# Combining two expert outputs per token: no zeroes ahead of the first store, and the first two tokens stored by themselves

## The chip, the cores and the metric

The kernel runs on one core of a Trainium2 chip. The metric is the device time of one execution in microseconds (us). Three runs of the kernel before took 238.85, 238.95 and 239.05 us, a median of 238.95. Smaller is better.

## The reference

Each of 16 x 1024 tokens has two rows of 512 float32 numbers (one from each of two experts) and two weights. The result is the weighted sum of the two rows:

```python
batch, seq, hidden, n_experts, k = 16, 1024, 512, 8, 2
# expert_outputs: (batch, seq, k, hidden), combine_weights: (batch, seq, k)
weights = combine_weights[..., np.newaxis]
return np.sum(expert_outputs * weights, axis=2).astype(np.float32)
```

Per token that is 4 KB in, 2 KB out, two multiplications and one addition for each output number. Over 16384 tokens 67.1 MB are read and 33.6 MB are written.

## The kernel before

**Tiling.** The tokens lie 128 to a "column": every one of the 128 partitions handles 128 tokens of its own. Those 128 are cut into ten tiles of `TILES = [13, 13, 12, 13, 13, 13, 12, 13, 13, 13]` tokens per partition. Tokens 0 to 114 of a partition are neighbours in memory (`main` is 115); the last tile's 13 come from a second region of the tensor. On the chip there is one large buffer, `et`, with four rooms (13, 13, 12 and 13 tokens a partition). Tile g goes into room g modulo 4, so it can be loaded when what was stored from that room has left it. `halves` is a second view of the same buffer in units of one 512-number row; a token takes two such rows.

**Order.** It is written out by hand; no planner changes it. There are two DMA queues here. The one that SyncE issues for (q1 in the profile; the profile writes SP for SyncE) takes all loads of expert outputs (line 76) and the last two stores. The one that ScalarE issues for (q10; ACT) takes the weights and the first seven stores (line 130). The start is:

1. VectorE clears `zt`, 16 x 128 numbers (line 108), and ScalarE issues a DMA that writes those 8 KB of zeroes to 16 places spread over the output (line 111). The stores overwrite them later.
2. ScalarE issues the weights: one DMA of 115 KB for tokens 0 to 114 (line 79) and two of 6.5 KB for the last tile (line 114). Then it loads its function table with one small operation (line 115).
3. Beside that SyncE issues the loads of the first four tiles, in five pieces, `FIRST = [2, 11, 13, 12, 13]`: two tokens, then the other eleven of tile 0, then tiles 1, 2 and 3. The first piece is cut into runs of 4 KB (`max_dma_last_dim`), so that each of its DMA rows is 4 KB long; in the others a row is all that a partition gets, 44 to 52 KB.

**Steps of a tile.** For tiles 0 to 7 (`WHOLE`) VectorE multiplies the whole room by the weights, in place (line 88), and then adds the two rows of each token into the front half of the room (line 97). The ScalarE queue then issues the store of the room, and SyncE the load of the tile four later, which waits until that store has landed. Tile 8 (`MIXED`) shares the products: VectorE takes the second row of all 13 tokens and the first row of three (lines 94 and 96), ScalarE the first row of the other ten (line 92). Tiles 7 and 8 leave in one store of 6.5 MB, whose issue waits for the sum of tile 8. The last tile goes token by token, ScalarE multiplying (line 102) and VectorE multiplying and adding (line 103), and leaves in the last store.

In this text L1 to L11 are the eleven loads in the order of their issue (L1: two tokens, L2: eleven, L3 to L11: tiles 1 to 9), S0 to S6 the stores of tiles 0 to 6, S78 that of tiles 7 and 8, and S9 the last.

**Semaphores.** The framework gives the DMAs eight semaphores in turn; a DMA that gets one that is still in use waits for the earlier owner. L5 gets that of the zeroes.

Of the kernel before, what the change touches and what calls it, by code (L numbers as in the profile page):

```python
# [1 line left out]

# [4 lines left out]


@with_exitstack
def kernel(  # L10
    ctx: ExitStack,  # L11
    tc: tile.TileContext,
    expert_outputs: bass.AP,
    combine_weights: bass.AP,
    out: bass.AP,
):

    nc = tc.nc
    b, s, k, h = expert_outputs.shape
    assert k == 2
    n = b * s
    P = nc.NUM_PARTITIONS
    per = n // P
    assert per * P == n

    ROOM = [13, 13, 12, 13]
    ROOMS = len(ROOM)  # L30
    SITE = [sum(ROOM[:i]) for i in range(ROOMS)]
    TILES = [13, 13, 12, 13, 13, 13, 12, 13, 13, 13]
    FIRST = [2, 11, 13, 12, 13]
    STORES = [[0], [1], [2], [3], [4], [5], [6], [7, 8], [9]]
    WHOLE = [0, 1, 2, 3, 4, 5, 6, 7]
    MIXED = [8]
    ALONE = 3
    FREE = {9: 0}
    LAST = 13
    assert all(c <= ROOM[g % ROOMS] for g, c in enumerate(TILES))  # L40
    assert sum(TILES) == per and [g for st in STORES for g in st] == list(range(len(TILES)))
    main = per - LAST
    starts = [sum(TILES[:g]) for g in range(len(TILES))]

    def rows(x):

        first = x[0 : P * main, :].rearrange("(p t) f -> p t f", p=P)
        second = x[P * main : n, :].rearrange("(p t) f -> p t f", p=P)
        return lambda t, c: first[:, t : t + c, :] if t < main else second[:, t - main : t - main + c, :]

    flat = out.rearrange("b s h -> (b s) h")
    eo = rows(expert_outputs.rearrange("b s k h -> (b s) (k h)"))
    cw = rows(combine_weights.rearrange("b s k -> (b s) k"))
    o = rows(flat)

    dt = mybir.dt.float32
    mult = mybir.AluOpType.mult
    add = mybir.AluOpType.add
    copy = mybir.ActivationFunctionType.Copy

    pool = ctx.enter_context(tc.tile_pool(name="all", bufs=1))
    et = pool.tile([P, sum(ROOM), k * h], dt)
    halves = et.rearrange("p j (k h) -> p (j k) h", k=k)
    wt = pool.tile([P, per * k], dt)
    wk = wt.rearrange("p (t k) -> p t k", k=k)
    zt = pool.tile([16, 128], dt)
    warm = pool.tile([P, 1], dt)

    def place(t):
        g = max(g for g in range(len(TILES)) if starts[g] <= t)  # L70
        return SITE[g % ROOMS] + t - starts[g]

    def load(t, c, **kw):
        at = place(t)
        assert place(t + c - 1) == at + c - 1
        nc.sync.dma_start(out=et[:, at : at + c], in_=eo(t, c), **kw)  # L76

    def weights(q, t, c):
        q.dma_start(out=wk[:, t : t + c, :], in_=cw(t, c))

    def combine(g, base):
        at, c, t0 = SITE[g % ROOMS], TILES[g], starts[g]
        if g in WHOLE or g in MIXED:
            room = halves[:, k * at : k * (at + c), :]
            x0, x1 = et[:, at : at + c, 0:h], et[:, at : at + c, h : 2 * h]
            if g in WHOLE:
                wb = wt[:, k * t0 : k * (t0 + c)].unsqueeze(2).to_broadcast([P, k * c, h])
                nc.vector.tensor_tensor(out=room, in0=room, in1=wb, op=mult)  # L88
            else:
                for i in range(ALONE, c):  # L90
                    x = et[:, at + i, 0:h]
                    nc.scalar.activation(out=x, in_=x, func=copy, scale=wt[:, k * (t0 + i) : k * (t0 + i) + 1])  # L92
                w1 = wk[:, t0 : t0 + c, 1:2].to_broadcast([P, c, h])
                nc.vector.tensor_tensor(out=x1, in0=x1, in1=w1, op=mult)  # L94
                w0 = wk[:, t0 : t0 + ALONE, 0:1].to_broadcast([P, ALONE, h])
                nc.vector.tensor_tensor(out=x0[:, 0:ALONE], in0=x0[:, 0:ALONE], in1=w0, op=mult)  # L96
            nc.vector.tensor_tensor(out=halves[:, base : base + c, :], in0=x0, in1=x1, op=add)  # L97
            return
        for i in range(c):
            t = k * (t0 + i)  # L100
            x0, x1 = halves[:, k * (at + i), :], halves[:, k * (at + i) + 1, :]
            nc.scalar.activation(out=x0, in_=x0, func=copy, scale=wt[:, t : t + 1])  # L102
            nc.vector.scalar_tensor_tensor(  # L103
                out=halves[:, base + i, :], in0=x1, scalar=wt[:, t + 1 : t + 2], in1=x0, op0=mult, op1=add
            )

    with tc.manual_schedule():
        nc.vector.memset(zt, 0.0)  # L108

        ahead = flat[0 : P * main, :].rearrange("(q t) h -> q (t h)", q=16)  # L110
        nc.scalar.dma_start(out=ahead[:, 0:128], in_=zt)  # L111
        weights(nc.scalar, 0, main)
        for half in (slice(0, P // 2), slice(P // 2, P)):
            nc.scalar.dma_start(out=wk[half, main:per, :], in_=cw(main, per - main)[half])
        nc.scalar.activation(out=warm, in_=nc.const_aps.tensor(1.0, (P, 1), dt), func=copy)  # L115

        t = 0
        for i, c in enumerate(FIRST):
            load(t, c, **({"max_dma_last_dim": k * h * 4} if i == 0 else {}))
            t += c  # L120
        assert t == sum(TILES[:ROOMS])
        for j, st in enumerate(STORES):
            room = FREE.get(st[0], st[0] % ROOMS)
            base, c = SITE[room] * k, 0
            for g in st:
                combine(g, base + c)
                c += TILES[g]
            assert c <= k * ROOM[room]
            q = nc.sync if j in (7, 8) else nc.scalar
            q.dma_start(out=o(starts[st[0]], c), in_=halves[:, base : base + c, :])  # L130
            for g in st:
                if g + ROOMS < len(TILES):
                    load(starts[g + ROOMS], TILES[g + ROOMS])


# [1 line left out]
_INS = ['expert_outputs', 'combine_weights']  # L137
_OUTS = [((16, 1024, 512), 'float32')]


# [23 lines left out]
```

## Time and profile before

| what | us |
|---|---|
| median of three runs (238.85 to 239.05) | 238.95 |
| profiled execution, its span (its own total time is not listed beside it) | 237.1 |
| VectorE busy | 190.0 (80% of the span) |
| ScalarE busy | 15.8 (7%) |
| both DMA queues, share of the 16 DMA engines over the span | 75.9% + 23.0% |
| moved | 100.80 MB, 425 GB/s over the span |

The span is what the profiler saw between the first and the last instruction; what lies around it is 1.85 us, taken against the median of the runs. In the table by windows, the DMA share counts a DMA row (the profile calls it a packet) wholly in the window in which it starts. A window that is short beside a row can therefore show more than 1, or much less; a window that begins and ends where rows of all 16 engines do is exact. "Landing" is the time from the issue of a DMA to the last of its semaphore's updates.

### The profile page before, as it was taken

To read this page: it belongs to the slowest core of one execution; us is meant where nothing else is said; L and a number is where in the kernel's file an instruction comes from. 1 tells how busy PE (TensorE), PEld (TensorE's weight loads), DVE (VectorE), ACT (ScalarE), POOL (GpSimd) and SP (SyncE) were. 2 spreads that over 40 slices of the span, in tenths; PEclk is the share of its full clock that TensorE was granted. 3 is DMA by queue.
4 is the path that set the end of the run, shared out by engine and by line. 5 is a ranking of instruction groups with operands and counts; after the bars stand their busy time and mean duration, and the time that the engine had idled before them with its cause. 6 is when DMAs were issued, how large, how long until landed. Compare 5 with 4: busy or idle time off the path is not lost.

```text
span 237.1 us, 154 instructions
## 1 busy us (share of the span) xinstructions
DVE 190.0 (80%) x33; ACT 15.8 (7%) x25; POOL 0.2 (0%) x4
## 2 busy tenths in 40 slices
DVE  0006999999999999999999998998499969919400
ACT  2000000000000000000000000000000055019200
POOL 0000000000000000000000000000000000000000
DMA  8999999989999999999899999999899999899996
GB/s 300 388 481 434 432 421 398 470 348 485 449 431 458 431 440 390 486 420 420 359 492 409 409 509 392 431 503 431 359 431 503 420 397 483 381 431 431 431 431 287
DMA packets 3344, 100.80 MB, mean 425 GB/s; under 512 B 512, under 2 KB 656, under 8 KB 912
## 3 DMA queue, kind: packets, MB, share of 16 engines
q1 hardware_dynamic: 2000, 77.33, 75.9%
q10 hardware_dynamic: 1344, 23.47, 23.0%
HBM read 67.24 MB, written 33.56 MB: 425 GB/s over the span
## 4 chain that ended last, share of the span: by engine, by line
DVE 55%; DMA 36%; issue 1%; ACT 0%; DVEq 0%; ACTq 0%; SPq 0%
DVE et L88 35%; DVE et L97 17%; DMA out_dram<-et 17%; DMA et<-in_expert_outputs_dram 12%; DMA wt<-in_combine_weights_dram 8%; DVE et L103 3%; ACT et L102 0%; DVEq L159 0%; ACTq L111 0%; DVE zt L108 0%; DVEq L88 0%; SPq L76 0%; ACTq L102 0%
## 5 line engine op out<-in xcount | busy, mean ns | idle before, releaser
L88 DVE TENSOR_TENSOR et<-et,wt 128x13312 f32<-128x13312 f32 (+1 forms) x8 | 110.0, 13754 | 23.8 <-DMA wt<-in_combine_weights_dram 18.7
L97 DVE TENSOR_TENSOR et<-et 128x6656 f32<-128x6656 f32 (+1 forms) x9 | 62.8, 6973 | 0.4
L92 ACT ACTIVATE et<-et,wt 128x512 f32<-128x512 f32 x10 | 6.2, 708 | 188.0 <-DMA et<-in_expert_outputs_dram 188.0
L103 DVE SCALAR_TENSOR_TENSOR et<-et,wt 128x512 f32<-128x512 f32 x13 | 8.7, 747 | 5.0 <-ACT et L102 5.0
L102 ACT ACTIVATE et<-et,wt 128x512 f32<-128x512 f32 x13 | 8.1, 707 | 14.0 <-DMA et<-in_expert_outputs_dram 14.0
L94 DVE TENSOR_TENSOR et<-et,wt 128x6656 f32<-128x6656 f32 x1 | 7.1, 7093 | 2.3 <-DMA et<-in_expert_outputs_dram 2.3
L96 DVE TENSOR_TENSOR et<-et,wt 128x1536 f32<-128x1536 f32 x1 | 1.8, 1751 | 0.0
L115 ACT ACT_TABLE_LOAD x1 | 1.3, 1283 | 3.1 <-issue 3.1
L108 DVE MEMSET zt<- 16x128 f32 x1 | 0.2, 165 | 0.8 <-PEq L148 0.8
L115 ACT ACTIVATE warm<-const-float32-1.0 128x1 f32<-128x1 f32 x1 | 0.2, 203 | 0.0
L148 POOL MEMSET const-bfloat16-1.0<- 128x1 bf16 x1 | 0.1, 102 | 0.0
L148 POOL MEMSET const-uint8-127<- 128x1 uint8 x1 | 0.1, 101 | 0.0
L148 POOL MEMSET const-float32-0.0<- 128x1 f32 x1 | 0.1, 99 | 0.2 <-issue 0.2
L148 POOL MEMSET const-float32-1.0<- 128x1 f32 x1 | 0.1, 98 | 0.0
## 6 DMA issues: line engine op xcount, KB each, us to landing
et<-in_expert_outputs_dram SPq DMA_DIRECT2D x7, 6656.0 KB, 32.2
out_dram<-et ACTq DMA_DIRECT2D x5, 3328.0 KB, 34.7
et<-in_expert_outputs_dram SPq DMA_DIRECT2D x2, 6144.0 KB, 41.1
out_dram<-et SPq DMA_DIRECT2D x1, 6656.0 KB, 19.9
out_dram<-et ACTq DMA_DIRECT2D x2, 3072.0 KB, 37.2
et<-in_expert_outputs_dram SPq DMA_DIRECT2D x1, 5632.0 KB, 18.2
out_dram<-et SPq DMA_DIRECT2D x1, 3328.0 KB, 14.0
et<-in_expert_outputs_dram SPq DMA_DIRECT2D x1, 1024.0 KB, 5.0
```

The costliest lines, as they stand in the source:

```text
L88: nc.vector.tensor_tensor(out=room, in0=room, in1=wb, op=mult)
L92: nc.scalar.activation(out=x, in_=x, func=copy, scale=wt[:, k * (t0 + i) : k * (t0 + i) + 1])
L94: nc.vector.tensor_tensor(out=x1, in0=x1, in1=w1, op=mult)
L96: nc.vector.tensor_tensor(out=x0[:, 0:ALONE], in0=x0[:, 0:ALONE], in1=w0, op=mult)
L97: nc.vector.tensor_tensor(out=halves[:, base : base + c, :], in0=x0, in1=x1, op=add)
L102: nc.scalar.activation(out=x0, in_=x0, func=copy, scale=wt[:, t : t + 1])
L103: nc.vector.scalar_tensor_tensor(out=halves[:, base + i, :], in0=x1, scalar=wt[:, t + 1 : t + 2], in1=x0, op0=mult, op1=add)
L108: nc.vector.memset(zt, 0.0)
L115: nc.scalar.activation(out=warm, in_=nc.const_aps.tensor(1.0, (P, 1), dt), func=copy)
L148: nc = _bacc.Bacc("TRN2", target_bir_lowering=False, num_devices=1)
```

## The change

It does four things. The buffer `zt`, its clearing and the DMA of zeroes go. ScalarE's first instruction is now the DMA of the weights. Ahead of the loop over tiles, the two tokens of L1 are multiplied, added and stored by themselves, the store through the ScalarE queue. For tile 0 the loop then multiplies, adds and stores the other eleven tokens only. The helpers `products`, `sums` and `store` hold what was written out before; for the tiles from 1 on they issue the same instructions.

```diff
-    zt = pool.tile([16, 128], dt)
...
+    def products(room, t, c):
+        wb = wt[:, k * t : k * (t + c)].unsqueeze(2).to_broadcast([P, k * c, h])
+        nc.vector.tensor_tensor(out=room, in0=room, in1=wb, op=mult)
+
+    def sums(at, c, base):
+        x0, x1 = et[:, at : at + c, 0:h], et[:, at : at + c, h : 2 * h]
+        nc.vector.tensor_tensor(out=halves[:, base : base + c, :], in0=x0, in1=x1, op=add)
+
+    def combine(g, base, done=0):
+        at, c, t0 = SITE[g % ROOMS] + done, TILES[g] - done, starts[g] + done
+        if g in WHOLE:
+            products(halves[:, k * at : k * (at + c), :], t0, c)
+            sums(at, c, base)
+            return
...
+    def store(q, t, base, c):
+        q.dma_start(out=o(t, c), in_=halves[:, base : base + c, :])
+
     with tc.manual_schedule():
-        nc.vector.memset(zt, 0.0)
-
-        ahead = flat[0 : P * main, :].rearrange("(q t) h -> q (t h)", q=16)
-        nc.scalar.dma_start(out=ahead[:, 0:128], in_=zt)
         weights(nc.scalar, 0, main)
...
+        early = FIRST[0]
+        products(halves[:, k * SITE[0] : k * (SITE[0] + early), :], 0, early)
+        sums(SITE[0], early, k * SITE[0])
+        store(nc.scalar, 0, k * SITE[0], early)
         for j, st in enumerate(STORES):
             room = FREE.get(st[0], st[0] % ROOMS)
             base, c = SITE[room] * k, 0
+            done = early if j == 0 else 0
             for g in st:
-                combine(g, base + c)
+                combine(g, base + c + done, done)
                 c += TILES[g]
             assert c <= k * ROOM[room]
-            q = nc.sync if j in (7, 8) else nc.scalar
-            q.dma_start(out=o(starts[st[0]], c), in_=halves[:, base : base + c, :])
+            store(nc.sync if j in (7, 8) else nc.scalar, starts[st[0]] + done, base + done, c - done)
```

More of the change, by code (lines that the diff above doesn't have):

```diff
@@ L79, in weights @@
         q.dma_start(out=wk[:, t : t + c, :], in_=cw(t, c))
[L81 to L84, printed above, removed]
-            x0, x1 = et[:, at : at + c, 0:h], et[:, at : at + c, h : 2 * h]
[L86 to L97, printed above, removed]
+    def products(room, t, c):
+        wb = wt[:, k * t : k * (t + c)].unsqueeze(2).to_broadcast([P, k * c, h])
+        nc.vector.tensor_tensor(out=room, in0=room, in1=wb, op=mult)
```

9 lines of the change are left out of this document (added).

## The prediction

> **What bounds the kernel now.** I read first the 40 slices with the DMA rows, then the chain that ended last, then the DMA engines by windows, then the landings. On the profile's page:
>
> ```profile
> DVE  0006999999999999999999998998499969919400
> DMA  8999999989999999999899999999899999899996
> q1 hardware_dynamic: 2000, 77.33, 75.9%
> q10 hardware_dynamic: 1344, 23.47, 23.0%
> DVE 55%; DMA 36%; issue 1%; ACT 0%; DVEq 0%; ACTq 0%; SPq 0%
> ```
>
> The chain gives 55% to VectorE, and would make it the bound. The slices say otherwise: VectorE has holes from the middle on, the DMA engines have none, and the two queues together fill 98.9% of 16 engines' time. The chain goes through VectorE only because each tile passes it. The DMA engines by windows, chosen so that rows of all engines begin and end at the edges (columns: window, its length, busy time of VectorE, ScalarE, GpSimd with counts, clock, DMA share, GB/s):
>
> ```profile
> 0.00:1.81 1.81, 0.17 (x1) 0.00 (x0) 0.20 (x4) 1.00 0.00 0
> 1.81:3.00 1.19, 0.00 (x0) 0.00 (x0) 0.00 (x0) 1.00 0.96 158
> 3.00:5.00 2.00, 0.00 (x0) 1.49 (x2) 0.00 (x0) 1.00 1.01 410
> 41.65:43.49 1.84, 1.84 (x1) 0.00 (x0) 0.00 (x0) 1.00 0.99 427
> 43.49:45.74 2.25, 2.25 (x1) 0.00 (x0) 0.00 (x0) 1.00 0.98 350
> 51.60:206.20 154.60, 146.92 (x17) 6.23 (x10) 0.00 (x0) 1.00 1.00 433
> 212.05:227.70 15.65, 8.71 (x13) 8.07 (x13) 0.00 (x0) 1.00 1.01 436
> 227.75:235.65 7.90, 0.00 (x0) 0.00 (x0) 0.00 (x0) 1.00 1.00 431
> 235.65:237.10 1.45, 0.00 (x0) 0.00 (x0) 0.00 (x0) 1.00 0.01 0
> ```
>
> From 51.60 to 235.65 us they are busy without a break at 431 to 436 GB/s, loads, stores or both. What is lost lies in four places: 1.81 us ahead of the first byte; a cold start, 1.19 us at 158 GB/s, which at 433 would take 0.43, so 0.75 us lost; 0.41 us (2.25 against 1.84) in the one round of rows of L4 just ahead of the first rows of S0, the first large store; 1.45 us behind the last byte. So the time is bytes over rate plus these four. VectorE's lead counts only where the DMA engines would run out of issued transfers.
>
> **The change part by part.** The rows on which the terms rest, in the order start, DMA issues, landings, VectorE:
>
> ```profile
> 0.73 4.52 SPq L76 DMA_DIRECT2D et<-in_expert_outputs_dram  x5
> 1.01 0.39 ACTq L111 DMA_DIRECT2D out_dram<-zt  x1
> 1.43 0.45 ACTq L79 DMA_DIRECT2D wt<-in_combine_weights_dram  x1
> L76 SPq DMA_DIRECT2D et<-in_expert_outputs_dram x11: 327/328/643, 0.7 to 183.9; - x11
> et<-in_expert_outputs_dram SPq DMA_DIRECT2D x1, 1024.0 KB, 5.0
> et<-in_expert_outputs_dram SPq DMA_DIRECT2D x1, 5632.0 KB, 18.2
> wt<-in_combine_weights_dram ACTq DMA_DIRECT2D x1, 115.0 KB, 18.2
> out_dram<-zt ACTq DMA_DIRECT2D x1, 8.0 KB, 3.9
> 19.73 14.04 DVE et L88
> 33.78 7.09 DVE et L97
> ```
>
> *Zeroes gone.* 8 KB at 433 GB/s are 0.02 us of DMA time. The clearing (0.17 us) was on an idle VectorE. L5's issue waited for the zeroes to land, at 1.01 + 3.9 = 4.9 us; it is now issued some 2 us sooner, worth nothing, since L2 to L4 (16.6 MB, 38 us at 433) are queued ahead of it. Sum: -0.02.
>
> *Weights first.* They move from 1.43 to about 0.73, beside L1's issue. Today their 115 KB need 18.2 us because each of their rows waits behind a row of L2 (a partition's 44 KB, 5632 KB over 128, take 1.66 us on one engine at 433/16 GB/s; eight per engine, 13 us). Now their eight rows per engine stand among L1's sixteen of 4 KB (0.16 us each at 410/16), so they should land with L1, at about 6 us. The bytes are the same. Two costs are not shown anywhere. First, two queues issue in the same moment: loads' issues took 0.33 to 0.64 us, so L1's may come up to 0.3 late with everything behind it, or not at all; I take 0.1, because L1 is likely to be past its issue before the other queue presses. Second, the cold start may be paid again for a second tensor: from 0 to +0.75, the loss in the window 1.81 to 3.00; below nothing by as much as 0.3, if two queues overlap their first latencies. I take 0, nearest to the rows after it, where L2 and the zeroes joined without a dip that the rates show (3.00:5.00 at 410).
>
> *Two tokens early.* VectorE: 2/13 of 14.04 and of 7.09, so 2.16 + 1.09 = 3.25 us, from about 6 to 9.4 us, where it idles today until 19.73. If that cover were gone (weights late, rival 4) it would cost nothing more than now, since the same 3.25 us are then inside tile 0. The store's issue follows on ScalarE's queue, where nothing waits behind it until S0; it is the ninth DMA, and the semaphore that it takes over is that of one of the first, all landed by then but for the weights in rival 4. On the DMA engines its 512 KB leave S0, so the bytes stay; as rows of 4 KB they go at 410 GB/s in place of 433: 1.28 - 1.21 = +0.07.
>
> *First large store.* The dip of 0.41 us ahead of S0 belongs, by place, to the first rows that are written in bulk; the zeroes ahead of it, 8 KB, did not prevent it. It should move to the early store, at about 10 us, among rows of L2. Bounds: -0.41 (small rows do not cause it, and S0 is then no longer the first) to +0.41 (paid at both). I take 0.
>
> *Tile 0 shorter.* It begins when L2 has landed, now at 19.73, then later by the early rows passed before it, about 5 of 8 per engine (0.8 us), and sooner by what the weights trail L2 today (at most 0.2): 20.4. Eleven thirteenths of 21.13 are 17.9 us, so S0 is issued at 38.3 where it was at 40.9. VectorE is then 2.6 us ahead, and S0, shorter by 2/13, lands about 4 us sooner. On busy DMA engines this buys nothing; it only changes who goes first. What it changes at the end is the next step.
>
> *Who is late next: S78.* The two queues alternate row by row, so stores that went ahead have pushed loads back. Ahead of tile 8's load (L10) there are then more store rows: the 1.28 us of the early store, and a third of 2.6 us (rows of stores are half as long as rows of loads), 0.9: 2.2, in whole rows of S0's kind (a partition's 26 KB, 0.98 us) two, so 2.0 us. The landings at the end:
>
> ```profile
> 192.63 7.09 DVE L94 TENSOR_TENSOR et<-et,wt 128x6656 f32<-128x6656 f32 x1 [2.30 <-DMA et<-in_expert_outputs_dram]
> 201.49 7.09 DVE L97 TENSOR_TENSOR et<-et 128x6656 f32<-128x6656 f32 x1
> 208.61 0.35 SPq L130 DMA_DIRECT2D out_dram<-et  x1
> 210.10:212.05 1.95, 0.00 (x0) 0.00 (x0) 0.00 (x0) 1.00 1.01 437
> 212.80 8.07 ACT L102 ACTIVATE et<-et,wt 128x512 f32<-128x512 f32 x13 [13.95 <-DMA et<-in_expert_outputs_dram]
> 222.29 0.34 SPq L130 DMA_DIRECT2D out_dram<-et  x1
> out_dram<-et SPq DMA_DIRECT2D x1, 6656.0 KB, 19.9
> out_dram<-et SPq DMA_DIRECT2D x1, 3328.0 KB, 14.0
> ```
>
> S78 is issued 16.0 us after VectorE got tile 8; from issue to first byte passes at most what L1 needed cold, 1.81 - 0.73 = 1.08. So today it is ready by 209.7, and its rows start when L11's end, at 212.05, both in q1: 2.4 us to spare. After: issued at 210.6, ready by 211.7, and L11 ends where the bytes put it, at 212.05 + 0.15. Still 0.5 us in hand, so 0; if it were three rows, 0.5 short. S9 has more: issued at 222.3, while S78's rows last to 227.7, 5.4 us.
>
> *Sum.* -0.02 + 0.1 + 0 + 0.07 + 0 + 0 + 0 = +0.15 us. The span goes from 237.1 to 237.25; with the same 1.85 around it, 239.1. What a measurement can tell from no change is about 0.2%, 0.48 us, so the forecast is "the same" (238.47 to 239.43).
>
> **The rivals.** *1. A dry spot ahead of S78* (slower). Place: the end of L11's rows. It decides from the point where tile 8 lands more than 2.5 us later than now (195.1 instead of 192.6). Price: what is missing, 0.5 us for a third row of stores, 1.5 for a fourth: 239.6 to 240.6. For it: only half a microsecond is in hand. Against: 1.08 is the cold figure, and L11 moves back too whenever anything before it does. Chance 0.12.
>
> *2. Cold costs paid twice* (slower): without the zeroes the first write is a large one, amid L2, and S0's dip stays too (+0.41), or the weights pay a cold start of their own (+0.75 at most). 0.15 + 0.41 to 0.15 + 1.16 gives 239.5 to 240.3. For it: both losses sit at the first use of a direction. Against: the weights among L2 showed none. Chance 0.14.
>
> *3. The dip goes, and the starts overlap* (faster): -0.41 - 0.3 + 0.15 gives 238.4. For it: a store of small rows begins beside loads that are already in full flow. Against: S0 began so as well, and paid. Chance 0.10.
>
> *4. The change doesn't do what it says*: the weights still land behind L2, the early sum comes at 20 us, all is as before but for the split, 0.07: 239.0. For it: they took 18.2 us with an issue only 0.7 later, and the zeroes, issued at 1.01, took 3.9. Against: L1's rows last until about 5 us. Within the "same". Chance 0.10.
>
> *5. The chain is right* and VectorE's 2.6 us reach the end: 236.5. Against: not a gap from 51.60 to 235.65. Chance 0.03.
>
> *6. A transfer's fixed cost stands on the path*, so that splitting a store costs what L1 shows over its bytes: landing 5.0 less 1024 KB at 433 (2.4), 2.6 us: 241.7. Against: the share of 1.00 through all the changes of transfer. Chance 0.02. Beside it stands the Trainium skill, "SBUF — State Buffer", section "The DMA setup-cost knee": each DMA pays about 2 us whatever its size, and its summary of rules asks for one DMA, not several. By that figure, an estimate, the early store would bring 241.1. The trace shows such a cost only where nothing else is queued: 1.81 us at the start and 1.45 at the end.
>
> **How the numbers follow.** The forecast itself has 0.49. It and rival 4 are the same: 0.59. Faster: rivals 3 and 5, 0.13. Slower: 1, 2 and 6, 0.28. The likeliest alone runs from 238.6 to 239.4 (0.15 with the two bounds of the issue, and half of the dip either way). The range goes from rival 3 (238.4) to a little under the far ends of rivals 1 and 2 (240.0), leaving out rivals 5 and 6 and some 0.1 of the others.
>
> **What the profile after would show.** Weights landing with L1 in about 5 us, not 18.2. VectorE with a product of 2048 and a sum of 1024 numbers per partition between 6 and 10 us, and tile 0's at about 20. One round of rows that is 0.4 us too long, at 10 us and not at 44. Tile 8 reached at 194.6, S78 issued at 210.6, L11 landed at 212.9, no window without DMA between. I would be wrong through a gap in the DMA share at 212, a start of the first bytes later than 1.81, or a dip that is missing or doubled; a gain beyond 0.7 us would mean that the rate itself had risen.

## The result

The changed kernel takes 239.84 us (median of 21 runs, 239.24 to 240.33), the kernel before 238.90 us beside it. The ratio is 1.0036, with a 95% interval from 1.0029 to 1.0043: slower by 0.9 us. That lies inside the range (238.4 to 240.0), but it is not the forecast "the same" (up to 239.43): it is on the side that had a chance of 0.28, 0.7 us above the predicted 239.1. The profiled execution took 240.07 us, with a span of 238.3 us, 1.1 us more than before.

The page of the changed kernel: the slices of VectorE and of the DMA engines, the queues, the chain.

```profile
DVE  0506999999999699969996999899499969969500
DMA  8899999999999999999989999989999999979996
q1 hardware_dynamic: 2000, 77.33, 75.6%
q10 hardware_dynamic: 1456, 23.46, 23.0%
DMA 64%; DVE 29%; ACT 0%; DVEq 0%; issue 0%; SPq 0%; ACTq 0%
```

VectorE now has holes between its tiles from the start, and the chain, which before gave VectorE 55%, now gives it 29%: it waits for loads. The DMA row has a 7 near its end that was not there. The start in order of time, and the landings:

```profile
0.72 0.45 ACTq L78 DMA_DIRECT2D wt<-in_combine_weights_dram  x1
0.72 5.96 SPq L75 DMA_DIRECT2D et<-in_expert_outputs_dram  x5
6.44 2.29 DVE L82 TENSOR_TENSOR et<-et,wt 128x2048 f32<-128x2048 f32 x1 [6.44 <-DMA et<-in_expert_outputs_dram]
8.76 1.23 DVE L86 TENSOR_TENSOR et<-et 128x1024 f32<-128x1024 f32 x1
19.93 11.89 DVE L82 TENSOR_TENSOR et<-et,wt 128x11264 f32<-128x11264 f32 x1 [9.94 <-DMA et<-in_expert_outputs_dram]
et<-in_expert_outputs_dram SPq DMA_DIRECT2D x1, 1024.0 KB, 5.6
wt<-in_combine_weights_dram ACTq DMA_DIRECT2D x1, 115.0 KB, 4.6
out_dram<-et ACTq DMA_DIRECT2D x1, 512.0 KB, 28.2
```

The change does what it says. The weights land 4.6 us after their issue in place of 18.2, the early sum is done at 10 us. The first sign of a cost is L1: 5.6 us to its landing in place of 5.0. The end:

```profile
196.43 7.09 DVE L100 TENSOR_TENSOR et<-et,wt 128x6656 f32<-128x6656 f32 x1 [2.04 <-DMA et<-in_expert_outputs_dram]
212.42 11.36 SPq L114 DMA_DIRECT2D out_dram<-et  x2
213.94 8.09 ACT L108 ACTIVATE et<-et,wt 128x512 f32<-128x512 f32 x13 [11.27 <-DMA et<-in_expert_outputs_dram]
```

And the DMA engines by windows around it (columns as in the prediction):

```profile
54.00:210.00 156.00, 141.82 (x16) 6.25 (x10) 0.00 (x0) 1.00 1.00 434
210.20:212.20 2.00, 2.00 (x1) 0.00 (x0) 0.00 (x0) 1.00 0.98 426
212.20:213.26 1.06, 0.19 (x1) 0.00 (x0) 0.00 (x0) 1.00 0.13 50
229.00:236.90 7.90, 0.00 (x0) 0.00 (x0) 0.00 (x0) 1.00 1.00 431
```

Tile 8 is reached at 196.43 (192.63 before), 3.8 us later and not 2.0; S78 is issued at 212.42 (208.61), and between 212.20 and 213.26 only one row of data begins on 16 engines. At first sight that is rival 1, the dry spot. But look at the third line of the end: tile 9, L11, lands at 213.9 (212.8 before). The 1.1 us by which the whole span is longer are there already when L11 lands, ahead of anything that S78 does. Whether the gap is the loss had to be tried.

Two further numbers come from the records of single DMA rows in the trace. Every DMA here gives each of the 16 engines the same rows. The *spread* is the time between the first and the last of the 16 engines' completions of one DMA. The *dip* is the sum over all load rows from 34 to 55 us of what each took beyond the usual duration of its size (1.815 us for a row of 48 KB), divided by 16 engines.

| kernel | median us | L1 to landing | spread L1, L10 | dip |
|---|---|---|---|---|
| before | 238.9 | 5.0 | 0.33, 0.32 | 0.45 |
| changed | 239.84 | 5.6 | 0.75, 2.22 | 0.80 |

### The profile page after: what moved, and what is told of

Its sections match the earlier page's. It is cut to its first block, busy times and chain, and to the rows that moved or that the text cites. A ratio compares the mean times of both kernels' runs of the same rounds, so it can differ in the third digit from the quotient of the medians.

```text
span 238.3 us, 155 instructions
## 1 busy us (share of the span) xinstructions
DVE 190.4 (80%) x34; ACT 15.8 (7%) x25; POOL 0.2 (0%) x4
## 4 chain that ended last, share of the span: by engine, by line
DMA 64%; DVE 29%; ACT 0%; DVEq 0%; issue 0%; SPq 0%; ACTq 0%
DMA et<-in_expert_outputs_dram 38%; DMA out_dram<-et 26%; DVE et L82 17%; DVE et L86 8%; DVE et L109 3%; ACT et L108 0%; DVEq L168 0%; SPq L75 0%; DVEq L82 0%; ACTq L108 0%
## 5 line engine op out<-in xcount | busy, mean ns | idle before, releaser
L82 DVE TENSOR_TENSOR et<-et,wt 128x13312 f32<-128x13312 f32 (+3 forms) x9 | 110.2, 12246 | 28.2 <-DMA et<-in_expert_outputs_dram 28.2
L86 DVE TENSOR_TENSOR et<-et 128x6656 f32<-128x6656 f32 (+3 forms) x10 | 62.9, 6292 | 0.4
```

## The experiments

The theories. *1, the dry spot:* the gap ahead of S78 is the loss. *2 or B, the zeroes:* without an early write of zeroes the first stores cost more. *3 or A, out of step:* weights and loads that start together leave the engines out of step, and since every landing is that of the slowest engine, the slowest decides the end. *C:* the early store's small rows do that by themselves. The diffs show the lines that matter; other lines are left out where "..." stands. Each kernel is timed beside the kernel before (238.86 to 238.88 us in all groups).

**Fill the gap.** Tile 7 gets a store of its own, so that S78's first half is queued behind L11 long before it ends.

```diff
                 combine(g, base + c + done, done)
+                if j == 7:
+                    store(nc.sync, starts[g], base + c, TILES[g])
                 c += TILES[g]
...
-            store(nc.sync if j in (7, 8) else nc.scalar, starts[st[0]] + done, base + done, c - done)
+            if j != 7:
+                store(nc.sync if j == 8 else nc.scalar, starts[st[0]] + done, base + done, c - done)
```

> The changed kernel, but tile 7's rows leave in a store of their own as soon as its sum is done, so that a store is queued behind L11 from about 195 us on and not from 212. Theory 1 (the loss is the dry spot ahead of S78): the gap of 0.8 us at 212 to 214 us is gone, 239.0 us. Theory 2 (cold costs are paid twice at the start, the dry spot only shows what would have been lost anyway): 239.6 to 239.8 us.

Measured: 240.05 us, ratio 1.0046 (1.0033 to 1.0059). The gap is filled and nothing is gained. Windows and two rows of this kernel:

```profile
210.20:212.20 2.00, 1.95 (x1) 0.00 (x0) 0.00 (x0) 1.00 0.98 426
212.20:213.26 1.06, 0.00 (x0) 0.00 (x0) 0.00 (x0) 1.00 0.94 402
194.18 29.33 SPq L114 DMA_DIRECT2D out_dram<-et  x3
213.69 8.07 ACT L108 ACTIVATE et<-et,wt 128x512 f32<-128x512 f32 x13 [11.27 <-DMA et<-in_expert_outputs_dram]
```

The share in the window of the gap goes from 0.13 to 0.94, and L11 lands at 213.6, nearly as late as in the changed kernel. From there to the end of the span it takes 24.4 us in the kernel before, in the changed kernel and in this one alike, so that S78 holds up none of them. The engines' last completions, 0.16 us apart in the changed kernel, are 1.03 us apart here. In the gap the engines that were ahead had waited for S78, and the slowest, which finished L11 at 213.5, had not. Theory 1 falls for the changed kernel.

**Only the zeroes gone.** The kernel before without lines 108 to 111; its first DMA on ScalarE's queue is then the weights.

```diff
-    zt = pool.tile([16, 128], dt)
...
-        nc.vector.memset(zt, 0.0)
-
-        ahead = flat[0 : P * main, :].rearrange("(q t) h -> q (t h)", q=16)
-        nc.scalar.dma_start(out=ahead[:, 0:128], in_=zt)
         weights(nc.scalar, 0, main)
```

> The kernel before without the zeroes; the weights are thereby the first DMA, nothing is stored early. Theory 1: S0 leaves at 40.9 us, no store gets ahead of the loads, tile 8 lands at 192.5 us: 238.9 us, with the dip ahead of S0 at 0.4 us. Theory 2: with no write ahead of S0 the dip grows to 0.8 us: 239.3 us. Theory 3 (the 16 DMA engines fall out of step, by 2.3 us in place of 0.3, because weights and loads start together): the spread of L10's completions is 2 us or more here too, and L10 lands near 194.4.

Measured: 239.55 us, ratio 1.0022 (1.0014 to 1.0031). So a loss of about two thirds of the size (0.0022 of 0.0036) comes without any early sum or store. The landing of L1, and the windows around the first rows of S0:

```profile
et<-in_expert_outputs_dram SPq DMA_DIRECT2D x1, 1024.0 KB, 5.7
wt<-in_combine_weights_dram ACTq DMA_DIRECT2D x1, 115.0 KB, 4.8
41.60:43.40 1.80, 1.80 (x1) 0.00 (x0) 0.00 (x0) 1.00 0.97 410
43.40:45.90 2.50, 2.50 (x1) 0.00 (x0) 0.00 (x0) 1.00 1.07 378
45.90:48.70 2.80, 2.80 (x1) 0.00 (x0) 0.00 (x0) 1.00 0.93 358
```

L1 lands 0.7 us late, with a spread of 0.85 us, and the dip comes twice: once at 43.4 us and once a round later, at 46.8, 0.82 us in all (0.45 before). By the single rows, nearly every engine has a load row that is too long in both rounds. Theories 2 and 3 both allow this.

**The early sum, but one store.** The two early tokens are stored with the other eleven.

```diff
-        store(nc.scalar, 0, k * SITE[0], early)
...
-            store(..., starts[st[0]] + done, base + done, c - done)
+            store(..., starts[st[0]], base, c)
```

> The changed kernel, but the two early tokens are stored with the other eleven in one store at 38 us; they are only computed early. Theory 1: a third of the 3 us by which S0 is earlier is ahead of L10, not the 1.3 us of the early store: tile 8 lands 1 us later than before, S78 is issued at 209.6, no dry spot, 238.9 to 239.1 us. Theory 2: the dip is paid once, at S0, but without zeroes ahead, 239.3. Theory 3, if the engines are put out of step by the start: spread 2 us, tile 8 at 195, 239.3; if by the early store's small rows: spread 0.3.

Measured: 239.61 us, ratio 1.0028 (1.0018 to 1.0037); L1 5.6 us to its landing, dip 1.0 us in two parts. Beside no_zeroes the early sum costs nothing that can be told (0.06 us), and beside the changed kernel the early store some 0.2 us; the intervals of all three overlap.

**The zeroes back, in two places.** First ahead of the weights, as before, with the early sum and store kept; then in the kernel before, behind the first weights.

```diff
+    zt = pool.tile([16, 128], dt)
...
+        nc.vector.memset(zt, 0.0)
+        ahead = flat[0 : P * main, :].rearrange("(q t) h -> q (t h)", q=16)
+        nc.scalar.dma_start(out=ahead[:, 0:128], in_=zt)
         weights(nc.scalar, 0, main)
```

> The changed kernel with the zeroes back in their old place ahead of the weights: the weights land late, at 18 to 20 us, and the early sum and store come then. Theory 1: the early store's rows go out between 22 and 40 us in place of 18 to 36, S0 leaves at 41; only 1.3 us of stores get ahead, tile 8 lands 0 to 1 us later, 239.0 us. Theory 2: the dip ahead of the first large store is 0.4 us as before, 239.0. Theory 3, start: spread 0.3 us; small rows: spread 2 us and 239.6.

Measured: 240.17 us (239.18 to 240.98), ratio 1.0051 (1.0034 to 1.0068). The profiled run was the fastest, with the engines in step (spreads 0.33 and 0.41); the weights landed at 19 us and the early sum came then. What its slower runs did is not seen. But its start is that of the kernel before, and by the median it is 1.3 us slower: with the early sum and store, a loss comes also where the weights do not start beside L1.

```diff
-        nc.scalar.dma_start(out=ahead[:, 0:128], in_=zt)
         weights(nc.scalar, 0, main)
+        nc.scalar.dma_start(out=ahead[:, 0:128], in_=zt)
```

> The kernel before with the DMA of zeroes moved behind the first weights, so the weights start with L1 and the zeroes are still written. Theory A: L1's completions spread by 0.8 us, as without zeroes, and 239.5 us. Theory B: the dip ahead of S0 is 0.4 us and the time 238.9 to 239.1.

Measured: 239.62 us, ratio 1.0020 (1.0000 to 1.0039); L1 5.8 us to its landing, spread 0.84, dip 1.1 us although the zeroes were written. This speaks against theory B: by the median, writing them does not help, if they do not hold the weights back. But the interval begins at no change, and the profiled run is one of the slower.

**Hold the weights back, two tries.** Both are shown against no_zeroes. The first puts the warm-up ahead of the weights in ScalarE's program.

```diff
+        nc.scalar.activation(out=warm, in_=nc.const_aps.tensor(1.0, (P, 1), dt), func=copy)
         weights(nc.scalar, 0, main)
...
-        nc.scalar.activation(out=warm, in_=nc.const_aps.tensor(1.0, (P, 1), dt), func=copy)
```

> The kernel before without the zeroes (as no_zeroes), but ScalarE issues the weights behind its warm-up operation, at about 2.4 us and not 0.7. Theory A (weights beside L1's cold start put the 16 engines out of step, and the slowest decides the end): L1's completions spread by 0.33 us as before, the dip ahead of S0 is 0.4 us, 238.9 us. Theory B (the zeroes warmed the write path, their absence is the loss): spread 0.33, but the dip is 0.8 us and the time 239.3 to 239.5.

Measured: 239.62 us, ratio 1.0024 (1.0012 to 1.0036). The try misses its aim, as its rows show:

```profile
0.72 1.28 ACT L107 ACT_TABLE_LOAD   x1 [0.72 <-PEq L143]
0.79 0.40 ACTq L78 DMA_DIRECT2D wt<-in_combine_weights_dram  x1
```

The DMA is issued at 0.79, while the table load ahead of it still runs. So it is a second no_zeroes, with the same time. The second try makes the weights wait for VectorE:

```diff
+        nc.vector.memset(wt, 0.0)
+        nc.vector.memset(wt, 0.0)
         weights(nc.scalar, 0, main)
```

> The kernel before without the zeroes; VectorE clears the weights' tile twice first, and the weights' DMAs wait for that, so they are issued at about 1.2 to 1.4 us (1.43 before) though no zeroes are written. Theory A (weights and loads that start cold together leave the 16 engines out of step): L1's completions spread by 0.33 us, one dip of 0.4 us, 238.9 us. Theory B (the missing zeroes): one dip or two, 0.8 us in all, 239.3 to 239.6.

Measured: 238.92 us, ratio 1.0003 (0.9994 to 1.0012). Its rows and its L1:

```profile
0.85 0.27 DVE L107 MEMSET wt<- 128x256 f32 x1 [0.85 <-PEq L145]
1.24 0.27 DVE L108 MEMSET wt<- 128x256 f32 x1
1.54 0.38 ACTq L78 DMA_DIRECT2D wt<-in_combine_weights_dram  x1
et<-in_expert_outputs_dram SPq DMA_DIRECT2D x1, 1024.0 KB, 4.8
```

No zeroes are written, the weights are issued at 1.54, L1 lands in 4.8 us, the spread is 0.42 at L1 and 0.37 at L10, the dip comes once (0.6), and the whole loss of no_zeroes is gone. This decides between A and B for the kernel without early sums: what the zeroes did was to hold the weights back, by 0.7 us at the issue. Their first row then begins at 6.4 us (6.7 before), behind L1, and not at 2.4 as in no_zeroes, amid its cold start.

**All of the start on one queue.** Four kernels put the weights on SyncE's queue, where they cannot start beside L1. The first two keep the two small DMAs of weights (rows of 104 bytes) on ScalarE's queue, behind its warm-up; the first is the changed kernel otherwise, the second no_zeroes.

```diff
             load(t, c, **({"max_dma_last_dim": k * h * 4} if i == 0 else {}))
+            if i == 0:
+                weights(nc.sync, 0, main)
```

> The changed kernel, with the first weights on SyncE's queue right behind L1, and ScalarE's two small ones behind its warm-up, so that nothing is read beside L1's cold start and the weights still land by about 6 us. Theory A: spread 0.33 us at L1, early sum at 6.5 us, early store as in the changed kernel; engines in step, so tile 8 lands 2.0 us later than before (194.6) and there is no dry spot; 239.0 to 239.1. Theory B: dip 0.8 us, 239.4 to 239.8. If the early store's small rows by themselves put the engines out of step, L3's completions spread by over 0.8 us and the time stays near 239.8.

> The kernel before without zeroes and without early sums, with the first weights on SyncE's queue behind L1. Theory A: spread 0.33 us, dip 0.4 us, 238.85 us. Theory B: dip 0.8 us, 239.3.

Measured: 240.26 us, ratio 1.0048 (1.0032 to 1.0065), and 239.96 us, 1.0040 (1.0028 to 1.0052). The spread is 0.34 and 0.43 at L1, but 0.80 and 0.86 at L2 and about 1 from L4 on. The two small DMAs, which were now issued at 0.79, began their rows at 4.6 us, beside the end of L1 and the first rows of L2; that they are what put the engines out of step was not tried apart. Not the 239.0 of theory A, and no case for B either, since the dip of the first was 0.57, one part only. The spread does not give the size of the loss: the second kernel has 1 us of it and loses 1.1 us, no_zeroes has 1.3 and loses 0.7. The next two put all of the start on SyncE's queue, the small ones last, and the weights ahead of L1 in the first of them and behind it in the second:

```diff
...
         assert t == sum(TILES[:ROOMS])
+        for half in (slice(0, P // 2), slice(P // 2, P)):
+            nc.sync.dma_start(out=wk[half, main:per, :], in_=cw(main, per - main)[half])
```

> The changed kernel, but all DMAs of the start are on SyncE's queue, in the order weights, L1, L2 to L5, the two small ones: no second queue beside the cold start, and the weights there by 6 us. Theory A: L1's spread 0.33 us, and 239.0 to 239.1 us, if the early store's small rows leave the engines in step; L1's rows begin up to 0.45 us later, of which the cold start that the weights' rows pay gives back a part: up to 239.4. Theory C (the early store's rows by themselves put the engines out of step): spread 0.33 at L1 but 1 us or more from L4 on, 239.5 to 240.2.

> As one_queue_weights_first, but L1 ahead of the weights. Theory A: as there, with L1 at its old place: 239.0 us. Theory C: spread 0.33 at L1, 1 us or more from L4 on, 239.5 to 240.2.

Measured: 241.82 us (240.17 to 243.24), ratio 1.0114 (1.0078 to 1.0150), and 242.31 us (239.92 to 243.37), 1.0125 (1.0077 to 1.0173). Both theories miss. The weights ahead of L1 in one queue leave a spread of 0.84 us at L1 too; L1 ahead of them leaves 0.32. One_queue_weights_first has the largest dry spot:

```profile
wt<-in_combine_weights_dram SPq DMA_DIRECT2D x2, 6.5 KB, 73.9
199.61 7.09 DVE L100 TENSOR_TENSOR et<-et,wt 128x6656 f32<-128x6656 f32 x1 [2.29 <-DMA et<-in_expert_outputs_dram]
215.59 10.47 SPq L114 DMA_DIRECT2D out_dram<-et  x2
212.50:216.60 4.10, 3.06 (x1) 0.36 (x1) 0.00 (x0) 1.00 0.52 221
```

Tile 8 comes at 199.6, S78 at 215.6, and for 4 us half of the DMA time is empty; summed over single rows the engines stand idle for 3.8 us each. Most of that falls to engines that were ahead: L10's completions lie 5.3 us apart, and L11 lands at 216.1, 3.4 us later than before, ahead of what S78 does. From there to the end it takes 25.3 us in place of 24.4, so the dry spot itself costs 0.9. In the profiled run of one_queue_l1_first (239.97 us) the engines stay in step (0.46 us), and it costs the same: L11 lands at 212.9, 0.1 later than before, the engines stand idle for 0.9 us each, and 25.3 us follow. So the mechanism of rival 1 exists, and it costs time when S78's rows are not there yet when the slowest engine ends L11. The small weights, which landed at 85 and 90 us in the first of the two and at 82 in the second, have a part in that: they stood in the loads' queue behind L5. Between the last rows of L5 and the first of L6 each engine runs 4 rows of stores in both kernels, and 2 in the changed one: two of the eight small rows of an engine took a turn against a row of 26 KB each, at 79 and 80 us, and most of the others ran in a bunch at 81. The last kernel takes them out of that queue:

```diff
         store(nc.scalar, 0, k * SITE[0], early)
+        for half in (slice(0, P // 2), slice(P // 2, P)):
+            nc.scalar.dma_start(out=wk[half, main:per, :], in_=cw(main, per - main)[half])
```

> As one_queue_l1_first, but the two small DMAs of weights are issued on ScalarE's queue behind the early store, so that no rows of 104 bytes stand in the loads' queue, where each of them lets a row of a store go ahead. The changed kernel without its start. If the loss of the changed kernel is the start (engines out of step), and the 3 us of gap in one_queue_weights_first came from the small rows: spread 0.3 to 0.5 us to the end, tile 8 at 194.6 to 195, no gap at 212, 239.0 to 239.2 us. If the early store by itself is harmful: tile 8 at 196 or later, a gap of 0.8 us or more at 212, and 239.7 or more.

Measured: 240.68 us (238.89 to 241.08), ratio 1.0061 (1.0041 to 1.0081). The profiled run was the 238.89 one:

```profile
et<-in_expert_outputs_dram SPq DMA_DIRECT2D x1, 1024.0 KB, 4.8
192.58 7.09 DVE L100 TENSOR_TENSOR et<-et,wt 128x6656 f32<-128x6656 f32 x1 [2.25 <-DMA et<-in_expert_outputs_dram]
208.56 14.05 SPq L114 DMA_DIRECT2D out_dram<-et  x2
```

Early sum and early store are both there, L1 lands in 4.8 us, the spread stays at 0.3, one dip of 0.6, and the time is that of the kernel before. That is the time theory A asks for, though not its way: tile 8 comes at 192.6, as before, and not at 194.6. And only two of nine runs are below 239.2, and five are above 240.6; no profile shows these. What makes the same program go one way or the other stays open.

No version beats the kernel before: weights_wait equals it. But the five kernels that keep the early sum and store, and have the first weights behind the zeroes or on SyncE's queue, are all slower than the changed kernel by their medians (240.17 to 242.31 against 239.84). So holding the weights back has won the loss back only where nothing is computed or stored early. What the early store costs by itself, and why, is not shown: the early sum without the early store was not run with the weights held back, and of the kernels that come nearest, zeroes_then_early and small_weights_behind, the profiled run was the fastest.

## Why the prediction was right or wrong

**In the range, by another way.** The forecast was "the same", which with rival 4 had a chance of 0.59, and the kernel is slower by 0.9 us, with no change outside the interval. The time lies in the range because this took in parts of rivals 1 and 2. It falls to rival 2 (239.5 to 240.3, chance 0.14), costs paid again at the start and at S0, though not quite as rival 2 has them; rival 3 is out, since neither the start nor the dip became shorter. Of the three signs of being wrong, two came: a gap at 212 and a dip about doubled; the first bytes came at 1.81 as before.

**Right: the bound, and VectorE's lead.** From 54 to 210 us the DMA engines run at 434 GB/s, as before. VectorE was 3 us ahead at S0 (issued at 37.9, forecast 38.3) and nothing of that reached the end. Rivals 4 and 5 are out: the weights did come early, and the chain's 2.6 us did not come.

**Wrong in size: "Weights first".** The step gave 0.1 us for the joint issue and took 0 of 0 to 0.75 for a second cold start, "nearest to the rows after it, where L2 and the zeroes joined without a dip". Those rows came after the cold start; the weights' first rows now run inside it, from 2.3 us on. L1 lands 0.6 to 1.0 us later in every kernel where the weights start beside it on the other queue (5.6 to 5.8 against 4.7 to 5.0). Of that, 0.34 are the weights' own rows (eight per engine of 0.042 us), which before ran among L2. At L3's end no_zeroes is 0.34 us late at its slowest engine, after the second dip 0.5 to 0.6, and at the end of its last store 0.67. The whole term is 0.63 us by the medians of no_zeroes and weights_wait, with the second dip in it. That is shown for no_zeroes; in the changed kernel, which has the same start, the term was not taken out by itself.

**Wrong: "First large store".** The dip did not move to the early store; rows of 4 KB passed without one, and S0 paid as before. In the changed kernel it is 0.80 against 0.45 us. The upper bound of the step (+0.41, paid twice) came true in size, but in another place: not at early store and S0, but all at S0, in rounds that follow each other. Over the profiled runs it goes with the spread, loosely: the five with a spread below 0.5 us at L4 have dips of 0.34 to 0.69 us, the other nine, at about 1 us or more, 0.57 to 1.09; why the first bulk rows cost at all was not tried.

**Half right: "Who is late next".** Counted at the first engine, L10's last row begins at 190.9 where it began at 188.9: two store rows, 2.0 us, as forecast. It lands 3.8 us later, and the other 1.9 us are the spread, 2.2 us in place of 0.3: the step took 16 engines for one. The Trainium skill, "DMA: Bandwidth & Descriptors", section "Why a DMA increments its semaphore by 16 and not by 1", says that a DMA's engines finish independently and that only the full count means that all data has landed. The trace agrees: L10's completions run from 194.1 to 196.3, and tile 8 starts at 196.4.

**Rival 1 seen, and not the cause.** The gap is there (0.8 us for the mean engine), where rival 1 put it, and filling it gave nothing. It cost only engines that were ahead; where the slowest had to wait too, in the two one_queue kernels, it cost 0.9 us.

**Rival 6.** Nothing here shows a fixed cost per transfer: tile7_apart has one DMA more than the changed kernel and is 0.2 us slower, within the intervals, not 2.6.

**Two slips that cost nothing.** In "Zeroes gone", L2 to L4 are 18.9 MB, 43.6 us at 433 GB/s, and not 16.6 MB and 38 us. And L5 is issued at 6.4 us, after L1 and the weights have landed, and not sooner than the 4.9 of before. Neither matters, with L2 and L3 queued until 36 us.

So the sum, as an estimate from the profiled runs: L11 lands 1.1 us later than before; about 0.3 from the start (as in no_zeroes), 0.35 from the larger dip, 0.1 from the split of S0 (0.07 by the forecast, not tried apart). Some 0.3 are the early store's, or chance: the changed kernel and one_store differ by 0.23, within their intervals. The shares were not taken out one by one, and the kernels that kept the early store without this start did not win theirs back. So the cause is shown for the loss of no_zeroes, and open in part for that of the changed kernel.

## What to carry to other kernels

When all DMA engines are busy to the end, look at the slowest of them and not at their mean: a landing is the last of 16, and a gap that only the faster ones see costs nothing. Something useless that stands ahead of a transfer may be holding it back to a better moment; before it is taken out, ask what then starts beside what. And where two queues alternate row by row, a tiny row can take a whole turn, as two of eight did here; so keep small rows out of the queue that must not fall behind.

## What was not expected of the hardware

- ScalarE issues a DMA at 0.79 us that stands in its program behind an operation with a table load (0.72, 1.28 us long): here the issue did not wait for the engine's earlier work.
- Once out of step, the engines stay so: in the changed kernel the spread of the loads is 2.1 to 2.3 us from L4 at 55 us to L10 at 194. At L11 it is 1.3 (1.0 in tile7_apart, without the gap), and behind the gap, at the last store, 0.16.
- The two kernels that start in step and store nothing early, weights_wait and the kernel before, repeat nearly always within 0.2% (weights_wait: 238.85 to 239.22; of the kernel before 3 of 100 runs are further off); the others scatter (small_weights_behind: 238.89 to 241.08), so that one profile shows one of several courses.
